# The last token block's key scans move into the last loop, with a third buffer for the second factors

## The chip, the cores and the metric

The kernel runs on one core of one Trainium2 chip. The metric is the time of one execution in device microseconds (us). The times of the kernel before are 2137.34, 2130.71 and 2142.05 us; their median is 2137.34 us.

## The reference, cut to what matters

One layer of a hybrid encoder: a mixer (HGRN2 and Hyena branches), then PEER, a retrieval among 128 x 128 single-neuron experts. The change touches PEER alone. For 512 tokens in blocks of 128:

```python
def block(xb):                                   # xb: 128 tokens x 1024
    qh = (xb @ w_q).reshape(T, 8, 2, 128)        # 8 heads, two halves each
    s = einsum('thpc,hpnc->thpn', qh, subkeys)   # 128 scores per half-head
    s1, i1 = top_k(s[:, :, 0], 16)
    s2, i2 = top_k(s[:, :, 1], 16)
    cand_s = s1[..., :, None] + s2[..., None, :] # 16 x 16 pairs
    top_s, pos = top_k(cand_s, 16)
    experts = take(i1 * 128 + i2, pos)
    g = softmax(top_s)
    u, v = u_tab[experts], v_tab[experts]        # 16,384 x 1024 tables
    act = gelu(einsum('td,thkd->thk', xb, u)) * g
    return einsum('thk,thkd->td', act, v)
```

The result is added to the residual and normed once more. All of it is float32.

## The kernel before, in words

The program is written by hand as nested generators. The order of the code sets priorities; a planner then orders each engine's queue by these priorities and by its own estimate of when operands and buffers are ready, so an instruction can be queued ahead of code that stands before it. Each queue is worked off in order. A pool's `bufs` is the number of buffers a name has; a new tile waits until the last reader of the buffer that it takes over is done. Matrices are split into a high and a low part (`split`, L83 to L86: ACT casts the high part, DVE or POOL subtracts), and each product is three products of parts (`mm3`, L89 to L97).

The four token blocks are treated in two ways. Block 0 (`GTB`) is *gathered*: for each of its 128 chosen pairs (8 heads x 16) a row of the u table per token is fetched by an indirect DMA of POOL and dotted with the token on DVE (L924), then a row of the v table is fetched and summed with its weight (L933). Blocks 1 to 3 (`DTB`) are *dense*: all 128 rows of 128 experts go through PE. A dense row's first product (`act_row`: uT row times the tokens, 24 products of 384 columns) and ACT's gelu give half of a pair `gact`; the second part (`combine`, 18 products of 512 columns) multiplies gated gacts with the v row into PSUM.

PEER runs in these stages:

- `projected` makes the normed tokens. Then `queries` (L1079) walks over 16 half-heads (head and half): it loads and splits a weight (`wlo` on DVE), projects, has PE make the scores of all four blocks, copies them by ACT into `s` (L1093), and has DVE scan each block with `top16` (L1239): the eight best, their indices, a copy without them (`rest`), the next eight, their indices, five operations per block. From half-head 8 on it takes one step after each half-head of the early selections (`chosen`, which is `select`) of the first two dense blocks.
- The gate stage finishes the dense selections and, in `gates_out`, makes for each token a 128 x 128 matrix of gates from one-hot products, which goes out to `Gd` in DRAM. A `fill` of dense first products is woven in: 2 x `KEPT` + `RING` - `LEFT` rows, 27. Of these pairs, `KEPT` are sent to DRAM (`kept`) and the others wait in the `ring`, which has `RING` / 2 + 1 buffers of one pair.
- The last loop weaves two generators: `rows` walks over the 128 dense rows and gives a weight per row, 6.0 for the first two and 2.25 for the others; `gathered` takes one step per unit of weight. `rows` does the dense first products still open (three ahead, 98 in the loop), splits v rows three ahead (`split_v`: SP loads `vraw`, ACT casts `vh`, DVE subtracts `vl`), multiplies pairs with their gates (`gated`: `gact` times `gt`, then `gh` and `gl`; a kept pair is first fetched into `gkept`) and combines. `gathered` does block 0's two selections (7 steps each, with the pool `slw2` of one buffer per name), turns the expert numbers into `gidx` (L912), and then takes one gather per step, 256 in all. In the loop POOL also does `ul`, the low part of the u rows, and all loads of `uraw`, `vraw`, `gt` and `gkept` are issued by SP, in one queue.
- The residual is added, normed and sent out.

Of the kernel before, what the change touches and what calls it, by code (L numbers as in the profile page):

```python
# [9 lines left out]
F32 = mybir.dt.float32  # L10
# [11 lines left out]
P = 128  # L22
L = 512
D = 1024
KB = D // P
TB = L // P
HEADS = 8
# [50 lines left out]
def run(gen):  # L78
    for _ in gen:
        pass  # L80


def split(nc, hi, lo, src, eng=None):  # L83

    nc.scalar.copy(hi, src)  # L85
    return (eng or nc.vector).tensor_sub(lo, src, hi).ins  # L86
# [49 lines left out]
def proj(C, src, xh, xl, eng=None):  # L136

    hi, lo = load_w(C, src, eng=eng)
    ps = C.ps_mm.tile([P, L], F32, name="ps_mm")
    mm3(C.nc, ps, [((hi[:, k], lo[:, k]), (xh[:, k], xl[:, k])) for k in range(KB)])  # L140
    return ps
# [17 lines left out]
def block_kernel(tc, a):  # L159

    nc = tc.nc
    with ExitStack() as ctx:
        const = ctx.enter_context(tc.tile_pool(name="const", bufs=1))
        ident = const.tile([P, P], F32, name="ident")
        ones = const.tile([P, P], F32, name="ones")
        nc.vector.memset(ones, 1.0)
        vec = const.tile([P, NVEC], F32, name="vec")
        nc.scalar.dma_start(vec, a["vec"])
        nc.scalar.dma_start(ident, a["ident"])
        epsc = const.tile([P, 1], F32, name="epsc")  # L170
        nc.vector.memset(epsc, EPS)
        C = Ctx()
        C.nc, C.tc, C.a, C.ident, C.ones, C.vec, C.eps = nc, tc, a, ident, ones, vec, epsc
        C.outer = ctx
        dp = ctx.enter_context(tc.tile_pool(name="dram", bufs=1, space=DRAM))
        C.Gd = dp.tile([12, P, P * 32], F32, name="Gd")
        C.hd = dp.tile([L, D], F32, name="hd")
        C.kept = dp.tile([KEPT, P, 2, ND], F32, name="kept")
        mh, ml = mixer(C)
        with ExitStack() as pctx:  # L180
            peer(C, pctx, mh, ml)
# [604 lines left out]
GTB = 0  # L786
DTB = (1, 2, 3)
ND = len(DTB) * P
T0 = DTB[0] * P
RING = 16  # L790
KEPT = 7
LEFT = 3
UB = 2
EARLY = 2
# [15 lines left out]
def peer(C, ctx, mh, ml):  # L810
    nc, tc, a = C.nc, C.tc, C.a
    cp = ctx.enter_context(tc.tile_pool(name="prc", bufs=1, side="right"))
    xh = cp.tile([P, KB, L], F32R, name="pxh")
    xl = cp.tile([P, KB, L], F32R, name="pxl")
# [3 lines left out]
    v16 = cp.tile([P, TB, 16, TOPK], F32, name="v16")  # L818
    i16 = cp.tile([P, TB, 16, TOPK], U32, name="i16")
# [10 lines left out]
    def chosen(pool, tb, part, ahead=2):  # L830
        return select(C, pool, tb, part, v16, i16, gate, eid, pio, ahead)

    projected(C, mh, ml, xh, xl, xg)
    rowctx = ExitStack()
    ring = rowctx.enter_context(tc.tile_pool(name="ring", bufs=RING // 2 + 1, side="right"))
    puctx = ExitStack()
    pu = puctx.enter_context(tc.tile_pool(name="pu", bufs=UB, side="right"))
    acts, factors, looping = {}, {}, []
    anchor = [None]
    last_gelu = [None]  # L840
# [11 lines left out]
    def act_row():  # L852

        r = order.pop(0)
        if r not in factors:
            split_u(r)
        if order:
            split_u(order[0])
        uh, ul = factors.pop(r)
        pa = C.ps_row.tile([P, 512], F32, name=C.ps_row_name)  # L860
        mm3(nc, pa[:, :ND], [((uh[:, k], ul[:, k]), (xh[:, k, T0 : T0 + ND], xl[:, k, T0 : T0 + ND])) for k in range(KB)])
        if r % 2 == 0:
            acts[r // 2] = ring.tile([P, 2, ND], F32, name="gact")
        g = acts[r // 2]
        last_gelu[0] = nc.scalar.activation(g[:, r % 2], pa[:, :ND], AF.Gelu_apprx_tanh).ins  # L865
        if r % 2 and r // 2 in kept:
            nc.scalar.dma_start(C.kept[kept.index(r // 2)], acts.pop(r // 2))

    NP = NK // 2
    kept = [p for p in range(NP) if (p + 1) * KEPT // NP > p * KEPT // NP]  # L870
    order = [r for r in range(NK) if r // 2 in kept] + [r for r in range(NK) if r // 2 not in kept]

    def act_rows():
        for _ in range(2 * KEPT + RING - LEFT):
            act_row()
            yield

    fill = act_rows()
    C.ps_row, C.ps_row_name = C.ps_mm, "ps_mm"
    queries(C, xh, xl, v16, i16, chosen, fill)  # L880
    C.wctx.close()
    C.ps_row, C.ps_row_name = ctx.enter_context(tc.tile_pool(name="ps_a", bufs=2, space=PSUM)), "ps_a"
    with tc.tile_pool(name="slw", bufs=2) as sw, tc.tile_pool(name="gb", bufs=1) as gb, \
# [10 lines left out]
    pv = rowctx.enter_context(tc.tile_pool(name="pv", bufs=2))  # L894
    swctx = ExitStack()
    sw = swctx.enter_context(tc.tile_pool(name="slw2", bufs=1))
# [4 lines left out]
    def gather(gp, tab, j):  # L901
        t = gp.tile([P, D], F32, name="grow")
        with tc.issue_after(anchor[0]):
            nc.gpsimd.indirect_dma_start(out=t, out_offset=None, in_=tab,  # L904
                                         in_offset=bass.IndirectOffsetOnAxis(ap=gidx[:, j : j + 1], axis=0))
        return t

    def gathered():

        yield from chosen(sw, GTB, 0, 1)  # L910
        yield from chosen(sw, GTB, 1, 1)
        nc.vector.tensor_copy(gidx, eid[:, GTB])  # L912
        swctx.close()
        gp = rowctx.enter_context(tc.tile_pool(name="gp", bufs=GBUFS))
        asked = chain(((a["u"], j) for j in range(P)), ((a["v"], j) for j in range(P)))
        there = [gather(gp, *q) for q in islice(asked, GAHEAD)]

        def row():
            there.extend(gather(gp, *q) for q in islice(asked, 1))
            return there.pop(0)  # L920

        for j in range(P):
            t = row()
            nc.vector.scalar_tensor_tensor(t, t, 1.0, xg, op0=ALU.mult, op1=ALU.mult, accum_out=gdot[:, j : j + 1])  # L924
            yield 1.2
        nc.scalar.activation(gw, gdot, AF.Gelu_apprx_tanh)
        nc.vector.tensor_mul(gw, gw, gate[:, GTB])
        for j in range(P):
            t = row()
            if j == 0:  # L930
                nc.vector.tensor_scalar(gacc, t, gw[:, 0:1], None, op0=ALU.mult)
            else:
                nc.vector.scalar_tensor_tensor(gacc, t, gw[:, j : j + 1], gacc, op0=ALU.mult, op1=ALU.add)  # L933
            yield 1.2
# [1 line left out]
    prep = {}  # L936

    def split_v(r):
        raw = pv.tile([P, D], F32, name="vraw")
        nc.sync.dma_start(raw, a["v"][r * P : r * P + P])  # L940
        vh = pv.tile([P, D], F32R, name="vh", bufs=AHEAD + 1)
        vl = pv.tile([P, D], F32R, name="vl", bufs=AHEAD + 1)
        split(nc, vh, vl, raw)
        prep[r] = vh, vl
# [69 lines left out]

    looping.append(True)
    weave(rows(), gathered(), 1.0)


# [57 lines left out]
    C.woctx.close()  # L1076


def queries(C, xh, xl, v16, i16, chosen, fill):  # L1079

    nc, tc, a = C.nc, C.tc, C.a
    with tc.tile_pool(name="slc", bufs=1) as cp, tc.tile_pool(name="slw0", bufs=2) as w2, tc.tile_pool(name="slw1", bufs=2) as sw:
        sk = cp.tile([P, 16, P], F32, name="sk")
        nc.scalar.dma_start(sk, a["skT"])

        def scores(hp, ps):
            qT = w2.tile([P, L], F32, name="qT")
            nc.scalar.copy(qT, ps)
            pt = C.ps_x.tile([P, 512], F32, name="ps_x")
            for tb in range(TB):  # L1090
                nc.tensor.matmul(pt[:, tb * P : tb * P + P], qT[:, tb * P : tb * P + P], sk[:, hp], start=True, stop=True)
            s = w2.tile([P, TB, P], F32, name="s")
            nc.scalar.copy(s, pt.rearrange("p (t n) -> p t n", t=TB))  # L1093
            for tb in DTB + (GTB,):
                top16(C, w2, v16[:, tb, hp], i16[:, tb, hp], s[:, tb])

        early = chain(*(chosen(sw, tb, 0) for tb in DTB[:EARLY]))
        for hp in range(16):
            scores(hp, C.first[hp] if hp < 2 else proj(C, a["w_q"][hp], xh, xl))
            if hp > 7:  # L1100
                run(islice(early, STEPS))
        run(early)
        for _ in range(2):
            next(fill)
# [134 lines left out]
def top16(C, pool, val, idx, src):  # L1239

    nc = C.nc
    rest = pool.tile(list(src.shape), F32, name="rest", tag=f"rest{src.shape[-1]}")
    nc.vector.max(val[:, 0:8], src)
    nc.vector.max_index(idx[:, 0:8], val[:, 0:8], src)
    nc.vector.match_replace(rest, val[:, 0:8], src, NEG)
    nc.vector.max(val[:, 8:16], rest)
    nc.vector.max_index(idx[:, 8:16], val[:, 8:16], rest)
# [111 lines left out]
```

## Time and profile before

| what | value |
|---|---|
| median of three runs | 2137.34 us (2130.71 to 2142.05) |
| the profiled execution | 2140.67 us, span 2138.9 us |
| PE busy | 2061.9 us, 96% |
| DVE busy | 1697.0 us, 79% |
| ACT busy | 962.4 us, 45% |
| POOL busy | 617.1 us, 29% |
| HBM traffic over the span | 189 GB/s |

Busy time is the share of the span in which an engine works on something; matmuls overlap in the records, so a busy PE need not be a PE at its peak. Where an engine was idle, the profile names what ended the wait. SPq is SP's queue of DMA issues. A name such as `vl` stands for all buffers of that name.

### The profile page before, as it was taken

How to read it: one execution, taken by the hardware profiler on the slowest of the kernel's cores; microseconds unless marked ns; L12 is line 12 of the kernel's file. 1: busy time of each engine (PE TensorE's matmuls, PEld its weight loads, DVE VectorE, ACT ScalarE, POOL GpSimd, SP SyncE). 2: the span in 40 equal slices, each digit the busy share in tenths (PEclk: the TensorE clock that was granted, in tenths of full speed). 3: DMA queues.
4: the chain of work that ended last, by engine and by line, in shares of the span. 5: the costliest groups of instructions: out<-in, count | busy, mean ns of one | idle time of the engine just before them, and what ended most of it. 6: DMA issues, size and time to landing. Idle time of an engine off the chain costs nothing.

```text
span 2138.9 us, 29773 instructions
## 1 busy us (share of the span) xinstructions
PE 2061.9 (96%) x11109; PEld 1819.3 (85%) x11109; DVE 1697.0 (79%) x3073; ACT 962.4 (45%) x1382; POOL 617.1 (29%) x361
## 2 busy tenths in 40 slices
PE   7999999999999999989989999999999999999998
PEld 6888888888888898778889888899888888899987
DVE  6788765999997648999999787787777668778765
ACT  5555435666565623337776332332332323332333
POOL 0000000000000000000001566777776666677640
PEclk9999999999999999989999999999999999999999
DMA  6212222221222434124547988888898888889964
GB/s 194 82 50 65 70 69 100 62 70 60 70 63 75 137 130 139 50 72 173 202 161 245 312 287 299 309 325 309 285 324 281 301 303 313 306 292 333 316 217 158
DMA packets 153661, 406.89 MB, mean 190 GB/s; under 512 B 12425, under 2 KB 65419, under 8 KB 151852
## 3 DMA queue, kind: packets, MB, share of 16 engines
q1 hardware_dynamic: 109884, 255.59, 35.5%
q0 software_dynamic: 36864, 134.23, 17.2%
q10 hardware_dynamic: 6768, 15.17, 2.0%
q8 instruction: 87, 1.43, 0.3%
q14 instruction: 58, 0.48, 0.1%
HBM read 372.83 MB, written 32.11 MB: 189 GB/s over the span
## 4 chain that ended last, share of the span: by engine, by line
PE 56%; DVE 20%; DMA 9%; issue 7%; ACT 4%; POOL 3%; DVEq 0%; ACTq 0%; POOLq 0%; SPq 0%
PE ps_mm L97 7%; PE ps_mm L95 7%; PE ps_mm L94 7%; PE acc L973 5%; PE acc L974 4%; PE acc L972 4%; PE ps_a L94 4%; PE ps_a L97 4%; PE ps_a L95 4%; DMA grow<-in_u,gidx 3%; DMA vraw<-in_v 3%; DMA grow<-in_v,gidx 2%; PE ps_g L1228 2%; POOL grow L904 2%; PE ps_x L718 2%
## 5 line engine op out<-in xcount | busy, mean ns | idle before, releaser
L86 POOL TENSOR_TENSOR ul<-uraw,uh 128x1024 fp32r<-128x1024 f32 x100 | 257.6, 2576 | 634.2 <-DMA uraw<-in_uT 396.4
L85 ACT CAST vh<-vraw 128x1024 fp32r<-128x1024 f32 x128 | 134.7, 1053 | 597.5 <-DMA vraw<-in_v 525.0
L94 PE MATMUL ps_a<-pxh,uh 128*128 128x384 f32 x1008 | 343.9, 341 | 23.6 <-ACT gact L865 23.4
L95 PE MATMUL ps_a<-pxl,uh 128*128 128x384 f32 x1008 | 342.3, 340 | 0.0
L973 PE MATMUL acc<-vl,gh 128*128 128x512 f32 x768 | 300.7, 392 | 0.4 <-DVE vl L86 0.4
L974 PE MATMUL acc<-vh,gl 128*128 128x512 f32 x768 | 300.8, 392 | 0.0
L972 PE MATMUL acc<-vh,gh 128*128 128x512 f32 x768 | 298.8, 389 | 0.0
L933 DVE SCALAR_TENSOR_TENSOR xg<-grow,gw,xg 128x1024 f32<-128x1024 f32 x127 | 194.9, 1534 | 88.6 <-DMA grow<-in_v,gidx 87.5
L94 PE MATMUL ps_mm<-xh,whi 128*128 128x512 f32 (+1 forms) x656 | 259.4, 397 | 1.6 <-ACT xh L195 1.3
L924 DVE SCALAR_TENSOR_TENSOR grow<-grow,xg 128x1024 f32<-128x1024 f32 x128 | 189.4, 1497 | 88.5 <-DMA grow<-in_u,gidx 88.5
L95 PE MATMUL ps_mm<-xl,whi 128*128 128x512 f32 (+1 forms) x656 | 255.2, 390 | 0.3 <-DVE xl L196 0.3
L94 PEld LDWEIGHTS ps_a<-pxh,uh 128*128 128x128 f32 x1008 | 191.1, 190 | 34.1 <-ACT gact L865 30.8
L826 POOL IOTA iota<- 128x512 bf16 x1 | 1.2, 1237 | 756.5 <-DVE gt L281 756.5
L97 PE MATMUL ps_a<-pxh,ul 128*128 128x384 f32 x1008 | 200.9, 340 | 10.7 <-DVE ul L86 10.3
L86 DVE TENSOR_TENSOR vl<-vraw,vh 128x1024 fp32r<-128x1024 f32 x128 | 188.9, 1477 | 18.9 <-ACT vh L85 18.8
L904 POOL DMA_INDIRECT grow<-in_u,gidx x128 | 185.8, 1451 | 45.3 <-issue 22.4
L95 PEld LDWEIGHTS ps_a<-pxl,uh 128*128 128x128 f32 x1008 | 191.1, 190 | 3.2
L97 PEld LDWEIGHTS ps_a<-pxh,ul 128*128 128x128 f32 x1008 | 177.7, 190 | 12.9 <-DVE ul L86 12.3
L904 POOL DMA_INDIRECT grow<-in_v,gidx x128 | 172.3, 1346 | 34.8 <-issue 18.6
L85 ACT CAST whi<-wraw 128x1024 fp32r<-128x1024 f32 x112 | 117.3, 1050 | 133.1 <-PE ps_mm L95 122.6
L974 PEld LDWEIGHTS acc<-vh,gl 128*128 128x128 f32 x768 | 144.1, 188 | 30.2
L973 PEld LDWEIGHTS acc<-vl,gh 128*128 128x128 f32 x768 | 144.1, 188 | 28.9 <-DVE vl L86 0.8
(413 smaller groups left out, 4150.3 us busy)
## 6 DMA issues: line engine op xcount, KB each, us to landing
uraw<-in_uT SPq DMA_DIRECT2D x128, 512.0 KB, 6.9
vraw<-in_v SPq DMA_DIRECT2D x128, 512.0 KB, 5.5
wraw<-in_w_in SPq DMA_DIRECT2D x80, 512.0 KB, 3.6
Gd<-Gs SPq DMA_DIRECT2D x12, 2048.0 KB, 7.3
gt<-Gd SPq DMA_DIRECT2D x32, 768.0 KB, 9.4
wraw<-in_w_q SPq DMA_DIRECT2D x16, 512.0 KB, 4.3
wraw<-in_w_b SPq DMA_DIRECT2D x8, 512.0 KB, 3.6
wraw<-in_w_a SPq DMA_DIRECT2D x8, 512.0 KB, 4.3
```

Of the source, the lines that this page charges most:

```text
L85: nc.scalar.copy(hi, src)
L86: return (eng or nc.vector).tensor_sub(lo, src, hi).ins
L94: nc.tensor.matmul(out, ah, bh, start=(i == 0), stop=False)
L95: nc.tensor.matmul(out, *((al, bh) if late else (ah, bl)), start=False, stop=False)
L97: nc.tensor.matmul(out, *((ah, bl) if late else (al, bh)), start=False, stop=(stop and i == n - 1))
L718: nc.tensor.matmul(pl[:, cs], KM[:, 0, cs], KM[:, 1, cs], start=True, stop=True)
L904: nc.gpsimd.indirect_dma_start(out=t, out_offset=None, in_=tab, in_offset=bass.IndirectOffsetOnAxis(ap=gidx[:, j : j + 1], axis=0))
L924: nc.vector.scalar_tensor_tensor(t, t, 1.0, xg, op0=ALU.mult, op1=ALU.mult, accum_out=gdot[:, j : j + 1])
L933: nc.vector.scalar_tensor_tensor(gacc, t, gw[:, j : j + 1], gacc, op0=ALU.mult, op1=ALU.add)
L972: nc.tensor.matmul(acc[k][:, c], gh[:, ts_], vh[:, ds_], start=(r == 0), stop=False)
L973: nc.tensor.matmul(acc[k][:, c], gh[:, ts_], vl[:, ds_], start=False, stop=False)
L974: nc.tensor.matmul(acc[k][:, c], gl[:, ts_], vh[:, ds_], start=False, stop=(r == NK - 1))
```

## The change

The scores of block 0 are no longer scanned in `queries`. ACT copies them into a tile `s0` that holds all 16 half-heads (8 KB per partition, from the start of the queries to the end of block 0's selections), and `s` holds the three dense blocks alone. `gathered` begins with the scans: eight half-heads, two per step, then the selection of the first four heads, then the same again. A weight that a generator yields counts only in the generator that leads the weave, so the 3.2 stands for one step. `vraw` gets three buffers where it had two. `RING` goes from 16 to 14 and `KEPT` from 7 to 8.

```diff
-RING = 16
-KEPT = 7
+RING = 14
+KEPT = 8
...
+    sgctx = ExitStack()
     pu = puctx.enter_context(tc.tile_pool(name="pu", bufs=UB, side="right"))
+    s0 = sgctx.enter_context(tc.tile_pool(name="sg", bufs=1, side="right")).tile([P, 16, P], F32, name="s0")
...
-    queries(C, xh, xl, v16, i16, chosen, fill)
+    queries(C, xh, xl, v16, i16, s0, chosen, fill)
...
     def gathered():
 
-        yield from chosen(sw, GTB, 0, 1)
-        yield from chosen(sw, GTB, 1, 1)
+        for part in range(2):
+            for hp in range(part * HEADS, part * HEADS + HEADS):
+                top16(C, sw, v16[:, GTB, hp], i16[:, GTB, hp], s0[:, hp])
+                if hp % 2:
+                    yield 3.2
+            yield from chosen(sw, GTB, part, 1)
+        sgctx.close()
...
     def split_v(r):
-        raw = pv.tile([P, D], F32, name="vraw")
+        raw = pv.tile([P, D], F32, name="vraw", bufs=3)
...
-            s = w2.tile([P, TB, P], F32, name="s")
-            nc.scalar.copy(s, pt.rearrange("p (t n) -> p t n", t=TB))
-            for tb in DTB + (GTB,):
-                top16(C, w2, v16[:, tb, hp], i16[:, tb, hp], s[:, tb])
+            pt = pt.rearrange("p (t n) -> p t n", t=TB)
+            s = w2.tile([P, len(DTB), P], F32, name="s")
+            nc.scalar.copy(s, pt[:, DTB[0] : DTB[-1] + 1])
+            nc.scalar.copy(s0[:, hp], pt[:, GTB])
+            for k, tb in enumerate(DTB):
+                top16(C, w2, v16[:, tb, hp], i16[:, tb, hp], s[:, k])
```

## Rows read from the trace of the kernel before

**Rows 1.** The page: busy time, share of the span and instructions of each engine

```profile
PE 2061.9 (96%) x11109; PEld 1819.3 (85%) x11109; DVE 1697.0 (79%) x3073; ACT 962.4 (45%) x1382; POOL 617.1 (29%) x361
```

**Rows 2.** Windows: length, busy us (count) of PE, PEld, DVE, ACT, POOL; clock, DMA share, GB/s

```profile
820.00:865.40 45.40, 45.40 (x227) 37.57 (x226) 45.09 (x260) 15.76 (x22) 0.00 (x0) 1.00 0.35 105
865.40:1143.40 278.00, 251.89 (x1602) 231.05 (x1601) 275.21 (x918) 173.46 (x285) 0.00 (x0) 0.97 0.39 143
...
1205.00:1215.00 10.00, 10.00 (x50) 8.87 (x50) 7.25 (x9) 2.50 (x4) 8.24 (x7) 1.00 1.03 404
1206.00:2076.00 870.00, 853.23 (x4234) 765.24 (x4232) 655.78 (x606) 279.51 (x351) 586.30 (x345) 1.00 0.86 304
```

**Rows 3.** Waits of PE, 865.4 to 1143.4: total us, times, longest us

```profile
PE ps_a L97 <- DVE ul L86: 10.3, 4, 7.9
```

**Rows 4.** Timeline of DVE in the queries: start us, length us, instruction

```profile
854.02 1.21 DVE L86 TENSOR_TENSOR wlo<-wraw,whi 128x1024 fp32r<-128x1024 f32 x1
...
860.09 1.21 DVE L86 TENSOR_TENSOR wlo<-wraw,whi 128x1024 fp32r<-128x1024 f32 x1
...
865.43 0.21 DVE L1134 CAST i16f<-i 128x128 f32<-128x128 uint32 x1
```

**Rows 5.** Timeline of ACT in the queries; in brackets the idle time before, and its end

```profile
854.07 0.59 ACT L1093 COPY s<-ps_x 128x512 f32<-128x512 f32 x1 [1.29 <-PE ps_x L1091]
...
860.54 0.59 ACT L1093 COPY s<-ps_x 128x512 f32<-128x512 f32 x1 [1.29 <-PE ps_x L1091]
```

**Rows 6.** Waits of PE for gact, from 1165 us on, and from 1200 us on

```profile
PE ps_a L94 <- ACT gact L865: 21.5, 14, 3.9
...
PE ps_a L94 <- ACT gact L865: 17.6, 13, 2.4
```

**Rows 7.** Timelines of DVE and PE at the entry of the last loop

```profile
1143.40 0.23 DVE L1134 CAST i16f<-i 128x128 f32<-128x128 uint32 x1 [0.69 <-PE ps_g L1228]
...
1169.40 0.49 PE L94 MATMUL ps_a<-pxh,uh 128*128 128x384 f32 x1 [3.90 <-ACT gact L865]
...
1199.14 0.22 DVE L912 CAST gidx<-eid 128x128 int32<-128x128 f32 x1
```

**Rows 8.** Waits of ACT, 1165 us to the end: the longest sum

```profile
ACT vh L85 <- DMA vraw<-in_v: 525.0, 96, 16.7
```

**Rows 9.** Waits of SP's queue, 1165 to 2100 us: the longest sum

```profile
SPq L940 <- DVE vl L86: 661.0, 119, 13.9
```

**Rows 10.** Timelines of ACT, POOL, PE and DVE around one stall of the last loop

```profile
1233.77 1.05 ACT L85 CAST vh<-vraw 128x1024 fp32r<-128x1024 f32 x1 [3.84 <-DMA vraw<-in_v]
...
1235.84 2.93 POOL L86 TENSOR_TENSOR ul<-uraw,uh 128x1024 fp32r<-128x1024 f32 x1 [1.95 <-ACT uh L85]
...
1236.21 0.44 PE L94 MATMUL ps_a<-pxh,uh 128*128 128x384 f32 x1 [2.05 <-ACT gact L865]
...
1236.45 3.40 DVE L86 TENSOR_TENSOR vl<-vraw,vh 128x1024 fp32r<-128x1024 f32 x1
```

**Rows 11.** DVE by shape, whole span: out<-in xcount | busy us, mean ns | idle before

```profile
L1247 DVE FIND_INDEX8 i<-v,rest 128x8 uint32<-128x128 f32 x64 | 18.5, 289 | 0.0
...
L1246 DVE MAX8 ctop<-rest 128x8 f32<-128x50 f32 x32 | 6.5, 202 | 0.1
```

**Rows 12.** DVE by line, last loop alone (1175 to 2093 us)

```profile
L86 DVE TENSOR_TENSOR vl<-vraw,vh 128x1024 fp32r<-128x1024 f32 x120 | 177.2, 1478 | 12.3 <-ACT vh L85 12.2
L959 DVE TENSOR_TENSOR gact<-gact,gt 128x768 f32<-128x768 f32 x55 | 67.3, 1225 | 10.3 <-DMA gt<-Gd 10.1
L86 DVE TENSOR_TENSOR gl<-gact,gh 128x768 fp32r<-128x768 f32 x55 | 65.5, 1190 | 0.0
...
L1246 DVE MAX8 ctop<-rest 128x8 f32<-128x50 f32 x4 | 0.8, 203 | 0.0
```

**Rows 13.** Timeline of DVE at the end: last gathered rows, first sums of PE's results

```profile
2073.04 2.60 DVE L933 SCALAR_TENSOR_TENSOR xg<-grow,gw,xg 128x1024 f32<-128x1024 f32 x2
...
2123.10 1.29 DVE L1028 TENSOR_TENSOR ht<-ht,acc 128x512 f32<-128x512 f32 x2 [5.85 <-PE acc L974]
```

More of the change, by code (lines that the diff above doesn't have):

```diff
@@ L1076, in projected, with queries @@
     C.woctx.close()
-def queries(C, xh, xl, v16, i16, chosen, fill):
+def queries(C, xh, xl, v16, i16, s0, chosen, fill):
     nc, tc, a = C.nc, C.tc, C.a
```

## The prediction

> **What bounds the kernel now.** I went from the page's share of each engine to windows cut at the stage borders, then to the waits of PE, of ACT and of SP's queue, and last to the timeline at the borders. On the page the reader is to see PE busy 2061.9 of the span's 2138.9 us [rows 1]: what can be won is PE's idle time, 77 us, and only where it lies. Two places of it are touched here.
>
> The first is the stretch from 865.4 to 1143.4 us, where pairs are selected and the dense blocks' gates are written out. DVE is busy 275.21 of 278.00 us there and PE 251.89 [rows 2], so DVE sets the end and PE has 26.1 us of idle; its longest sum of waits is for DVE's ul, 10.3 us in 4 [rows 3]. From 820 to 865.4 both look full [rows 2], but the timeline separates them: DVE takes 6.07 us from one half-head's wlo to the next (854.02 to 860.09) [rows 4], while ACT copies scores, as PE delivers them, 6.47 us apart (854.07 to 860.54) [rows 5]. The wlo gains on the copy from 0.05 to 0.45 us ahead, so in the first eight of 16 half-heads PE is the slower one. At 865.43 the first early selection begins on DVE [rows 4], and from there DVE has more to do than PE.
>
> The second is the last loop. From 1206 to 2076 us PE is busy 853.23 of 870.00 us at a granted clock of 1.00, DVE 655.78 us (75%), and the DMA engines 0.86 at 304 GB/s [rows 2]. PE is the bound, and its waits are nearly all of one sort, for gact, ACT's gelu: 21.5 us in 14 from 1165 on, of which 17.6 in 13 lie after 1200, none over 2.4 us [rows 6]; the other one, 3.90 us, is the entry [rows 7]. ACT is not loaded: it sat 525.0 us before vh until vraw landed [rows 8], with the gelu behind vh in its queue. SP, which issues vraw, sat 661.0 us in 119 waits for DVE's vl, the last reader of a vraw buffer [rows 9]. One case: ACT gets vraw at 1233.77 after 3.84 us, casts, runs the gelu, and PE goes on at 1236.21 after 2.05 us idle [rows 10].
>
> **The change part by part.** The sum is made against the profiled execution, 2140.67 us (span 2138.9 and 1.8 around it). It lies 3.3 us above the median of 2137.34, inside the spread of the three runs (2130.71 to 2142.05).
>
> *The gathered block's 16 scans leave the query stage.* Of a half-head's 6.07 us on DVE, wlo is 1.21 [rows 4]; four scans of five operations share the other 4.86, 1.215 us each. (By its duration one operation takes up to 0.289 us [rows 11] and a scan 1.45; successive ones overlap, so starts are the better measure.) Sixteen are 19.4 us. In the first eight half-heads PE sets the pace and nothing gets shorter. In the other eight DVE is behind without a break, and all that follows up to 1143.4 us moves ahead by 8 x 1.215 = 9.7 us. Bounds: 19.4 us, if DVE was the bound from the start; nothing, if the planner puts these scans, ready long before, back among the gate work. I take 9.7, because DVE is full there and PE has 26.1 us of idle to give. What is late next in that stretch is still DVE.
>
> *ACT copies scores in two pieces.* Sixteen copies of 128 x 128 are added, and a row of 128 x 512 took 0.59 us [rows 5], so under 9 us; the other piece gets shorter. ACT is busy 15.76 of 45.40 us in that stage [rows 2] and idle 1.29 us before each copy until PE is done [rows 5], which hides it: zero. If that cover goes, at most 0.59 us per half-head.
>
> *The scans come back at the entry of the last loop.* Before, DVE spends 55.8 us between the end of the gates (1143.40) and gidx (1199.14) [rows 7], on two selections and the first rows' factors. In code order the eight added yields move the first gather from row 2.9 of the loop to row 6.4: the first two rows take 6 steps each, every further row 2.25, and there are 22 steps ahead of the gathers where there were 14. A row's own work on DVE is 2.7 us: one vl of 1.48 and half of a pair's gact product and gl, 1.2 [rows 12]. So DVE reaches gidx 55.8 + 19.4 + 3.5 x 2.7 = 85 us after the gates. PE makes 4234 products in 870 us [rows 2], 0.2055 us each; a row with its dense partner has 24 + 18 of them, 8.6 us. It came to the loop 26 us after the gates (1169.40) [rows 7], so it is at row 6.4 after 26 + 55 = 81 us. DVE comes 4 us late, against factors that are split three rows (26 us) ahead. Before, by the same count, it was 5 us late (55.8 against 26 + 25), and PE did not wait there beyond the 3.90 us. Bounds: nothing, to 23 us (16 scans of 1.45 us, end to end, as their single rest buffer may force, on PE's path). I take 2, near the row of before.
>
> *The later gathers.* The last sum of a gathered row ended at 2075.6, and the last additions waited for PE until 2123.1 [rows 13]. 3.5 rows of 8.6 us later is 2106 on the old axis, 17 us short of PE's end: zero. If that cover went, each us beyond would count.
>
> *A third buffer for vraw.* A load can be issued a row sooner, 7.7 us on the mean (98 dense rows over 120 steps make 37.6 products a step). No stall in the loop is over 2.4 us, so where DMA has room each is covered; where the engines are full (1.03 at 404 GB/s from 1205 to 1215) [rows 2], a load issued earlier only queues earlier. Bounds: nothing to 17.6 us. I take two thirds, 12 us, because the mean share is 0.86, nearer to full than to free, yet the wait for vl stands in 119 of 128 loads.
>
> *Ring shorter by a pair, an eighth kept pair.* The fill stays at 27 dense rows (2 x 8 + 14 - 3), the entry does 3 and the loop 98, as before; counted through the code, a ring buffer is still used again no sooner than three rows after its release. One more pair of 384 KB goes out and comes back, 1.3 us of DMA each way at 304 GB/s, hidden. On SP's queue one more gkept, with its one buffer, may hold a vraw behind it, by no more than the longest wait there, 13.9 us [rows 9], against the row (7.7 us) now in hand: zero, up to 6 us if it meets a late one.
>
> Sum: 2140.67 - 9.7 - 12 + 2 = 2121; less the 3.3 us by which this execution lay above the median, 2117.7. I say 2118.
>
> **Two rules of the skill.** In the loop, DVE operations on two SBUF operands stretch beside POOL: vl took 3.40 us at 1236.45, while POOL's ul ran from 1235.84 for 2.93 us [rows 10]; its mean is 1478 ns there [rows 12]. The scans of one operand do not: 203 ns in the loop [rows 12], 202 over all [rows 11]. The Trainium skill says so in SBUF — State Buffer, § Who interferes with whom: a DVE instruction with two SBUF inputs and a GpSimd instruction that reads SBUF shut each other out, one with a single input is untouched. By it the moved scans cost the same 19.4 us in the loop; held up like vl they would cost 24. The page DMA: Bandwidth & Descriptors of the Trainium skill, § Where 436 GB/s comes from, speaks against the buffer: HBM gives a core about 358 GB/s, and 304 is 85% of that. The 404 GB/s of the row above stands over its figure, so the trace gives the loop more room than the page does.
>
> **The rivals.**
> A. *The buffer is hidden by DMA.* vraw is late because the DMA engines are full, and the stalls stay. For it: the share of 0.86, and 96 times that ACT waited for vraw [rows 8]. Against it: SP issues vraw only after vl in 119 cases [rows 9]. Time: 2137.3 - 9.7 + 2 = 2129.6.
> B. *The scans move and free nothing.* The planner's new order holds PE as long as before up to 1143. Against it: DVE is full there [rows 2]. Buffer alone: 2137.3 - 12 + 2 = 2127.3.
> C. *Both come in full.* 2137.3 - 9.7 - 17.6 = 2110; with some of the first eight half-heads' scans counted, 2104.
> D. *Slower: the entry of the loop starves.* The scans stand on DVE ahead of the first gact products, gl and vl; ACT's gh and the gelu behind it wait, and PE with them, as in the 3.90 us at 1169.40 [rows 7]. Price: 23 us on the path, less 9.7, with the buffer's gain used up by the transfers that bunch up behind it: 2137.3 + 13 = 2150. It decides once DVE is more than 26 us late at row 6.4, 22 more than I count. For it: the wait at the entry is there already. Against it: with 5 us of delay PE lost nothing more.
>
> **How the numbers follow.** Forecast (2112 to 2125) 0.42, C 0.14, A 0.18, B 0.14, D 0.12. A measurement can tell about 0.5%, 10.7 us, from no change, so faster means below 2126.6: the forecast, C and a third of A and B, which lie within 3 us of that line, 0.66. Within: the rest of A and B and a little of D, 0.24. Slower: 0.10. The range leaves out some of C and most of D: 2106 to 2139.
>
> **What would show it.** Right: DVE's end of the gates (1143.4) comes about 10 us sooner; SP's 661 us for vl shrink by hundreds, and PE's 17.6 us for gact fall to about 6; gidx comes some 30 us later after the loop's start than now, with no gap of PE over 4 us before the first gather. Wrong: the gates end where they did (first step); the waits for gact stay, with DMA at 0.86 or more (buffer); PE waits for vl, gh or gact around the new scans (entry); or the last gathered row is summed after PE's last product.

## The result, and the profile after

The changed kernel takes 2113.90 us (median of 5 runs, 2113.02 to 2115.41), a ratio of 0.9895 to the kernel before (95% interval 0.9871 to 0.9918). The forecast was 2118 us, in 2106 to 2139. Run once more with the later experiments it gave 2113.16 us, 0.9886 (0.9865 to 0.9906). The profiled executions stand 26.8 us apart (spans 2138.9 and 2112.1).

All comparisons of traces below use three borders: the first score product of the queries, the gates' end (DVE's last product `own` begins), and PE's last product. They lie at 818.8, 1140.9 and 2130.8 us before, at 818.4, 1131.9 and 2104.2 us after. So the stages in front became 8.6 us shorter (322.1 to 313.5), the rest 17.6 us (989.9 to 972.3). Line numbers after are 2 to 10 higher than before (L972 to L974 are now L979 to L981).

Windows of the kernel after (columns as in [rows 2]): the queries, the gate stage, the whole rest, the entry of the loop, and its two halves:

```profile
818.40:915.40 97.00, 93.88 (x469) 77.68 (x468) 91.44 (x515) 31.64 (x60) 0.00 (x0) 0.99 0.21 66
915.40:1131.90 216.50, 201.15 (x1351) 191.49 (x1351) 214.94 (x572) 154.70 (x258) 0.00 (x0) 0.96 0.48 176
1131.90:2104.20 972.30, 965.37 (x4801) 869.68 (x4800) 801.21 (x892) 350.54 (x428) 636.80 (x356) 0.99 0.84 297
1158.00:1168.00 10.00, 7.67 (x26) 6.68 (x27) 10.00 (x12) 7.31 (x9) 4.64 (x2) 0.66 0.50 163
1221.10:1631.00 409.90, 407.23 (x2023) 366.67 (x2023) 332.63 (x365) 143.82 (x170) 317.09 (x174) 1.00 0.90 321
1631.00:2061.60 430.60, 430.60 (x2152) 388.67 (x2152) 359.48 (x245) 152.86 (x180) 294.10 (x174) 1.00 0.87 309
```

The same window of the rest in the kernel before:

```profile
1140.90:2130.80 989.90, 967.89 (x4803) 868.49 (x4802) 749.28 (x802) 333.04 (x428) 615.63 (x356) 1.00 0.83 292
```

Length less busy time is PE's idle time: 22.0 us before, 6.9 after. In the loop's second half PE has no gap left. The waits of PE in that stretch after, where [rows 6] had 14 for gact:

```profile
PE acc L979 <- ACT vh L85: 2.6, 1, 2.6
PE ps_a L97 <- POOL ul L86: 2.2, 1, 2.2
PE acc L980 <- DVE vl L86: 2.1, 2, 1.6
```

ACT now waits for PE, and little for vraw [rows 8]; SP waits for vl about as long as ever [rows 9] (667.4 us before in the same stretch). ACT's waits, then SP's:

```profile
ACT vh L85 <- PE acc L981: 179.7, 54, 3.6
...
ACT vh L85 <- DMA vraw<-in_v: 70.7, 13, 10.9
```

```profile
SPq L947 <- DVE vl L86: 651.4, 121, 12.2
```

DVE's scan operations on `s` and `s0` (one name in the trace) from the first score product to the gates' end. The three dense blocks have 48 of each kind, so block 0 still has 14 first maxima and 12 index searches here; of its 80 operations 54 left the stage:

```profile
L1254 DVE FIND_INDEX8 i<-v,s 128x8 uint32<-128x128 f32 x60 | 17.2, 288 | 0.0
L1253 DVE MAX8 v<-s 128x8 f32<-128x128 f32 x62 | 16.1, 283 | 5.4 <-ACT s L1102 5.4
L1255 DVE MATCH_REPLACE8 rest<-v,s 128x128 f32<-128x128 f32 x48 | 13.4, 279 | 0.0
```

### The profile page after: what moved, and what is told of

Its sections match the earlier page's. It is cut to its first block, busy times and chain, and to the rows that moved or that the text cites. A ratio compares the mean times of both kernels' runs of the same rounds, so it can differ in the third digit from the quotient of the medians.

```text
span 2112.1 us, 29790 instructions
## 1 busy us (share of the span) xinstructions
PE 2058.7 (97%) x11109; PEld 1822.7 (86%) x11109; DVE 1736.1 (82%) x3073; ACT 978.6 (46%) x1396; POOL 638.2 (30%) x361
## 3 DMA queue, kind: packets, MB, share of 16 engines
q0 software_dynamic: 36864, 134.23, 17.6%
## 5 line engine op out<-in xcount | busy, mean ns | idle before, releaser
L86 POOL TENSOR_TENSOR ul<-uraw,uh 128x1024 fp32r<-128x1024 f32 x100 | 265.3, 2654 | 589.7 <-DMA uraw<-in_uT 387.6
L979 PE MATMUL acc<-vh,gh 128*128 128x512 f32 x768 | 299.7, 390 | 2.6 <-ACT vh L85 2.6
L981 PE MATMUL acc<-vh,gl 128*128 128x512 f32 x768 | 301.5, 393 | 0.0
L940 DVE SCALAR_TENSOR_TENSOR xg<-grow,gw,xg 128x1024 f32<-128x1024 f32 x127 | 208.6, 1643 | 63.1 <-DMA grow<-in_v,gidx 62.0
L931 DVE SCALAR_TENSOR_TENSOR grow<-grow,xg 128x1024 f32<-128x1024 f32 x128 | 195.9, 1541 | 73.6 <-DMA grow<-in_u,gidx 73.3
L906 POOL DMA_INDIRECT grow<-in_u,gidx x128 | 201.0, 1570 | 41.4 <-issue 19.4
L85 ACT CAST uh<-uraw 128x1024 fp32r<-128x1024 f32 x128 | 134.7, 1053 | 143.5 <-PE ps_a L95 76.5
```

The costliest lines, as they stand in the source:

```text
L979: nc.tensor.matmul(acc[k][:, c], gh[:, ts_], vh[:, ds_], start=(r == 0), stop=False)
L981: nc.tensor.matmul(acc[k][:, c], gl[:, ts_], vh[:, ds_], start=False, stop=(r == NK - 1))
```

## The experiments

Each kernel is compared with runs of the kernel before on its own chip. The 12 runs were made on more than one chip, where the kernel before had medians of 2135.5 to 2140.9 us, so ratios are what compares across groups.

**The parts one by one.** *Buffer*: the kernel before with the third buffer and the new ring, no scan moved.

```diff
-RING = 16
-KEPT = 7
+RING = 14
+KEPT = 8
...
-        raw = pv.tile([P, D], F32, name="vraw")
+        raw = pv.tile([P, D], F32, name="vraw", bufs=3)
```

> The third vraw buffer with RING 14 and KEPT 8, the scans left in the query stage. Theory (two separate gains that add: the scans shorten the stage that DVE bounds, the buffer takes the loop's stalls): 2122 us (2118 to 2127), ratio about 0.993; the gates end as before, within 2 us of 1141; ACT's wait for vraw falls from 525 us to under 120, PE's wait for gact in the loop from 17.6 to under 4 us. Rival (the loop got free because the gathers come later and in less crowded transfers, not because of the buffer): within 4 us of before, ACT's wait for vraw over 400 us.

2117.49 us, 0.9896 (0.9868 to 0.9925): more than I expected. The rest takes 966.5 us, 23.4 less than before:

```profile
1141.30:2107.80 966.50, 962.62 (x4805) 868.67 (x4803) 780.37 (x802) 351.76 (x428) 640.06 (x356) 1.00 0.84 299
```

Idle fell from 22.0 to 3.9 us (18.1), and the same products took 5.3 us less busy time. DMA moves 299 GB/s where it moved 292, and a vraw lands no sooner after its issue (median 6.2 us; 5.5 before), but ACT's wait for vraw is 53.6 us where it was 525.0: the engines had room for the earlier loads.

*Ring*: the ring alone (the two constants above).

> RING 14 and KEPT 8 alone. Theory: no change, 2137 us within 4, gact waits in the loop still 12 to 20 us. Rival (the new ring makes the planner lay the loop out in another way, and that is part of the gain): 5 us or more faster, with gact waits under 10 us.

2145.03 us, 1.0026 (1.0000 to 1.0052), at the edge of what I allowed. The new ring brings nothing by itself and may cost some 5 us beside two buffers. The ring of 16 with three buffers was not run, so the new ring's price there stays open.

*Scans*: the changed kernel with two vraw buffers.

> The changed kernel with vraw back at two buffers (scans moved, RING 14, KEPT 8). Theory: 2128 us (2124 to 2132), ratio about 0.996; the gates end 9 us sooner than before, PE's waits for gact in the loop stay at 12 to 20 us and ACT's for vraw over 400 us. Rival (the relief of DVE is the whole gain): 2114 us, like the changed kernel. Rival (the scans at the entry cost as much as they free): 2137 us.

2151.22 us, 1.0063 (1.0040 to 1.0086): a miss, and on the other side of the kernel before. *Scans16* puts the old ring back as well, so that only the scans are moved (against the changed kernel):

```diff
-RING = 14
-KEPT = 8
+RING = 16
+KEPT = 7
...
-        raw = pv.tile([P, D], F32, name="vraw", bufs=3)
+        raw = pv.tile([P, D], F32, name="vraw")
```

> The scans moved alone, with two vraw buffers and the ring of 16 with 7 kept pairs as in the kernel before. Theory one, the entry is what the moved scans cost and the old ring takes the rest of the loss away: 8.6 us gained at the gates, about 6 given back at the entry, 2135 to 2139. Theory two, late vraw loads and the scans meet at the entry whatever the ring, as in the scans kernel (6 us above the kernel before with the short ring, 2 with that ring's 4 taken off): 2142 to 2148.

2146.75 us, 1.0043 (1.0023 to 1.0062): theory two. The scans alone make the kernel slower, though its gates end 9.3 us sooner after the first score product (312.8). The rest, and PE's waits in it:

```profile
1130.50:2138.90 1008.40, 977.39 (x4801) 875.15 (x4800) 775.31 (x892) 333.72 (x428) 621.24 (x356) 0.98 0.81 286
```

```profile
PE ps_a L94 <- ACT gact L867: 18.8, 12, 3.7
PE acc L980 <- DVE vl L86: 7.2, 3, 5.6
```

It is 18.5 us longer than before, half by idle time (31.0 against 22.0) and half by longer busy time (977.4 against 967.9), at a granted clock of 0.98. With three buffers the same move costs the rest 5.8 us (972.3 against 966.5).

*Half*: the changed kernel, with block 0's first eight scans left in the queries.

```diff
-            for hp in range(part * HEADS, part * HEADS + HEADS):
+            for hp in range(HEADS, 2 * HEADS) if part else ():
...
+            if hp < HEADS:
+                top16(C, w2, v16[:, GTB, hp], i16[:, GTB, hp], s0[:, hp])
```

> The changed kernel, but the gathered block's first eight half-heads are scanned in the query stage again; only the other eight move. Theory (PE sets the pace in the first eight, so moving these gains nothing): 2114 us within 3, the gates end within 1.5 us of the changed kernel's, gidx some 10 us sooner. Rival (DVE was the bound from the start): half of the stage's gain is lost, the gates end 4 to 5 us later, 2118 to 2119 us.

2111.91 us, 0.9870 (0.9842 to 0.9899). The gates end 313.9 us after the first score product against 313.5: the first eight scans had gained nothing there.

**Is vraw late because DMA is full?** *Novgather*: the kernel before, with 127 of the 128 gathers of v rows left out; the sums take one row again and again.

```diff
-        asked = chain(((a["u"], j) for j in range(P)), ((a["v"], j) for j in range(P)))
+        asked = chain(((a["u"], j) for j in range(P)), ((a["v"], j) for j in range(1)))
...
-            t = row()
+            if j == 0:
+                t = row()
```

> The kernel before, without 127 of the 128 gathered rows of v: the sums use one row over and over, so only DMA load is taken from the loop's second half, about 0.5 MB every 8.6 us falls to half. Theory one (prediction's rival A: vraw is late because the DMA engines are full): ACT's waits for vraw in the second half fall by more than half, and PE's gact stalls after the last u row is gathered (1650 us) vanish. Theory two (the load is issued too late, for SP waits for vl): ACT still waits for vraw about as often, shorter by under a third, and some stalls after 1650 us stay.

One run: 2179.66 us, which neither theory had. The sums, no longer paced by gathers, fill DVE until 1907.5 us. That stretch here, and in the kernel before:

```profile
1640.40:1907.50 267.10, 236.34 (x1113) 205.99 (x1111) 264.18 (x183) 71.42 (x90) 67.53 (x24) 0.96 0.40 127
```

```profile
1640.40:1907.50 267.10, 261.83 (x1304) 235.10 (x1303) 201.41 (x145) 88.16 (x111) 177.62 (x106) 1.00 0.86 306
```

ACT's waits for vraw from 1640 to 1907 us here, and in the kernel before:

```profile
ACT vh L85 <- DMA vraw<-in_v: 153.2, 23, 10.0
```

```profile
ACT vh L85 <- DMA vraw<-in_v: 149.8, 25, 14.0
```

With DMA at 0.40 instead of 0.86, ACT waits for vraw as long. That alone doesn't clear DMA, for the edit also filled DVE (264.18 of 267.10 us), whose vl a load's issue waits for. But once the sums are done, DVE is over half free while DMA has a share of 0.48, and ACT's waits for vraw (here from 1907 to 2130 us) nearly vanish:

```profile
1907.50:2169.80 262.30, 258.77 (x1260) 231.14 (x1260) 112.49 (x87) 95.44 (x123) 58.94 (x24) 0.99 0.48 149
```

```profile
ACT vh L85 <- DMA vraw<-in_v: 11.2, 2, 8.8
```

Within this run the wait goes with DVE and not with DMA's share, as it should if a load is late because it is issued late, behind vl. That the DMA engines had room at 0.86 is shown by buffer, not by this run.

**Where the ring costs.** *Kept2*: the ring kernel with a second buffer for gkept.

```diff
-            g = pv.tile([P, 2, ND], F32, name="gkept", bufs=1)
+            g = pv.tile([P, 2, ND], F32, name="gkept", bufs=2)
```

> As the ring kernel (two vraw buffers, no scan moved, ring of 14 with 8 kept pairs), with a second buffer for gkept. Theory one, the 4 us that the ring kernel lay above the kernel before come from gkept's single buffer, which holds vraw loads behind it on SP's queue: SP's waits for DVE's gl ahead of gkept (36.4 us in 7 there) fall to under 5, and the time goes back to 2138, within 3. Theory two, they come from the ring itself or from chance: the waits fall, and the time stays at 2143, within 3.

2150.06 us, 1.0053 (1.0025 to 1.0081). SP's waits for gl didn't fall (33.6 us in 6; 36.4 in 7 in the ring kernel), so the edit did not take away what it was to test, and why the ring costs beside two buffers stays open.

**What the entry costs.** *Again*: the changed kernel, for comparison.

> The changed kernel once more, beside the others of this group. Both theories: 2114 us, within 3. It is here so that the next kernels are compared with it on one chip.

2113.16 us. *Halflate*: the half kernel with six empty steps before the gathered work.

```diff
     def gathered():
+        for _ in range(6):
+            yield
```

> As the half kernel (eight of the gathered block's scans stay in the queries, eight move), but the gathered work takes its first step in the loop six steps later. Theory one, the price at the entry is DVE's work standing ahead of the first gact product: the first product of the loop comes 6 us sooner after the gates than in the half kernel (38.5 us there), and the time falls to 2107, within 3. Theory two, the planner sets DVE's order whatever the code order of these steps, so the first product moves by under 2 us: 2112, within 3. A loss over 4 us would say that the gathered rows, some 20 us later, then reach the end of the loop.

2112.13 us, 0.9881 (0.9859 to 0.9903). The first product of the loop comes 37.6 us after the gates (38.5 in half), and PE waits 7.0 us for gact (6.9): theory two. The planner left DVE's work ahead of that product where it was; gidx came 77.0 us after the gates' end, only 4.8 later than in half.

*Behind*: the changed kernel, with the moved scans bound behind the first row's vl.

```diff
-                top16(C, sw, v16[:, GTB, hp], i16[:, GTB, hp], s0[:, hp])
+                with tc.issue_after(first[0]): top16(C, sw, v16[:, GTB, hp], i16[:, GTB, hp], s0[:, hp])
...
-    prep = {}
+    prep, first = {}, []
...
-        split(nc, vh, vl, raw)
+        first.append(split(nc, vh, vl, raw))
```

> The changed kernel, with the 16 moved scans held behind the first row's vl of the last loop, so that none of their operations runs in the query or gate stage and none ahead of the loop's first gact product, gl and vl. Theory one, the changed kernel loses 7 us at the loop's entry because DVE's scans stand ahead of the first factors, and left a third of the scans' operations in the earlier stages: gates end another 3 to 6 us sooner, PE waits under 4 us in all at the entry, gidx comes some 20 us later, nothing is lost at the end: 2104, within 4. Theory two, DVE is simply full at the entry and its work has to be done somewhere: the waits come back a few rows later for vl, gl or the exponentials in ACT's queue, as long as before: 2113, within 3.

2114.50 us, 0.9887 (0.9860 to 0.9913): no faster. From the gates' end at 1131.4 to 1234.8 us PE is never idle, so the order of DVE's queue was the price of the first rows. But gidx comes at 1234.8 us, and POOL's queue has gathers ahead of a ul. PE's only wait in the rest, and POOL's timeline at that place (start, length, instruction):

```profile
PE ps_a L97 <- POOL ul L86: 10.2, 1, 10.2
```

```profile
1235.27 1.09 POOL L906 DMA_INDIRECT grow<-in_u,gidx  x1 [7.61 <-DVE gidx L919]
...
1249.78 2.35 POOL L86 TENSOR_TENSOR ul<-uraw,uh 128x1024 fp32r<-128x1024 f32 x1
```

Nine gathers stand between the two. All 80 scan operations left the earlier stages here, and these took 313.4 us, as in the changed kernel (313.5): the last 26 gained nothing.

*Halfheld*: the half kernel, with scans and selections bound behind the first vl (the scans and `first` as in behind).

```diff
+    def held(gen):
+        for go in iter(int, 1):
+            with tc.issue_after(first[0]): c = next(gen, None)
+            if c is None: return
+            yield c
...
-            yield from chosen(sw, GTB, part, 1)
+            yield from held(chosen(sw, GTB, part, 1))
```

> As the half kernel, but the eight moved scans and both selections of the gathered block are held behind the first row's vl of the last loop. Theory one (the order of DVE's queue is the price): gates end as in the half kernel, the 6.9 us that PE waited for gact at the entry there shrink to under 2, 2105, within 3. Theory two (DVE is full whatever the order): 2112, within 3, with PE waiting for vl or gl after the first rows.

2124.92 us, 0.9942 (0.9919 to 0.9965). The wait for gact went (0.4 us), but gidx came 92.1 us after the gates' end (72.2 in half), and PE waits 20.5 us for a ul: neither theory. *Behind6*: the behind kernel with the first gathers six steps later.

```diff
         nc.vector.tensor_copy(gidx, eid[:, GTB])
+        for _ in range(6): yield 1.2
```

> As the behind kernel, with the first gathers six steps (some 23 us) later in code order, so that one more ul, the twelfth of the loop, stands ahead of them on POOL's queue. Theory one, in the behind kernel the time won at the loop's entry was lost again because POOL's first gather waits for gidx with the next ul behind it, and PE behind that for 10.2 us: that wait falls under 2 us, and the time is 2103, within 3. Theory two, the late selection is paid for in any case: another wait (for ul again, for vl, or the last gathered rows at the end) takes its place, 2110 or more.

2111.96 us, 0.9877 (0.9855 to 0.9898). One more ul runs ahead of the gathers, and PE still waits 7.2 us, for the one after it: theory two. Behind6, half, halflate and the changed kernel (0.9870 to 0.9895) can't be told apart.

## Why the prediction was right, step by step

**The scans leave the queries: 9.7 forecast, 8.6 measured**, with DVE still full in the gate stage (214.94 of 216.50 us) and no gain from the first eight, as half shows. What I had listed only as a bound happened in part: the planner put 26 of the 80 operations back among earlier work, those that need no `rest` buffer. It cost nothing, as behind shows. Of the 26, 14 lie before 864 us, where PE sets the pace. The other 12 lie where I took DVE for the bound; in behind, without them, DVE is idle for 10.8 us of the stages in front instead of 7.1, and nothing is gained. So DVE is no longer the only bound there, though I had said that it stays what is late next.

**ACT's copies: zero, as forecast.** They take 0.48 and 0.27 us by the trace, where one took 0.59 [rows 5].

**The entry of the loop: 2 forecast, 5.8 measured**, within the bounds. The trace of after shows two places. The first is the first row: ACT's exponentials of the new selection stand in its queue ahead of gh and vh (start, length, instruction, idle before it):

```profile
1156.00 0.26 ACT L1169 ACTIVATE ex<-ex 128x64 f32<-128x64 f32 x1 [6.43 <-DVE ex L1168]
1156.87 0.83 ACT L85 CAST gh<-gact 128x768 fp32r<-128x768 f32 x1 [0.61 <-DVE gact L966]
1157.61 1.99 ACT L85 CAST vh<-vraw 128x1024 fp32r<-128x1024 f32 x2
```

DVE, with scans and selection first, lets ACT wait 6.43 us; PE waits 2.6 us for vh and 1.6 for vl, and from 1158 to 1168 us has a clock of 0.66. But these 4.2 us take the place of the 3.9 us that PE waits for gact in the buffer kernel, as before [rows 7]. The second place is the first gather (POOL's timeline, then PE's):

```profile
1221.59 1.54 POOL L906 DMA_INDIRECT grow<-in_u,gidx  x1 [9.68 <-PE ps_a L97]
...
1228.12 2.35 POOL L86 TENSOR_TENSOR ul<-uraw,uh 128x1024 fp32r<-128x1024 f32 x1
```

```profile
1230.53 2.53 PE L97 MATMUL ps_a<-pxh,ul 128*128 128x384 f32 x8 [2.18 <-POOL ul L86]
```

This ul had its uh from ACT at 1213.0 us, but five gathers stand ahead of it, and the first of them waits for gidx. (The profile names a product of PE; gidx was done at 1221.30, 0.29 us before the gather, as it was 0.28 us before it in the kernel before.) Idle time in the rest is 3.0 us more than in the buffer kernel: 2.2 for this ul, 0.5 for a later vl, and only 0.3 at the first row. Busy time is 2.8 us more, and the clock covers it: busy time times the missing clock, summed over windows of 5 us, is 4.1 us in after and 1.5 in buffer, and some 1.5 us of the 4.1 follow this wait. So my count of rows looked near the right place, the first gather, but asked only whether DVE's factors are late there; late was POOL's ul, behind the gathers, a path that is in neither my sum nor a rival. Rival D named the wait of the first row, which hardly grew. The scan operations themselves didn't stretch, as forecast: three that run beside a ul of POOL, from 1143.75 us on, take 0.28 to 0.29 us.

**The later gathers: zero, as forecast.** gidx came 89.2 us after the gates' end, 31.0 more than before (29 forecast), and the last sum ended 42.6 us ahead of PE's last product (I had said 17).

**The third buffer: 12 forecast, 23 measured, past my bound of 17.6.** This is the term that was mis-sized, and the others hid it. All of the loop's stalls for gact behind the entry went, not two thirds: I cut them because I took 0.86 of DMA for nearly full, and buffer shows that it had room. The rule of the Trainium skill that spoke against the buffer (DMA: Bandwidth & Descriptors, § Where 436 GB/s comes from: some 358 GB/s from HBM for a core) did not come to bear: the changed loop's first half moves 321 GB/s at a share of 0.90, and PE has 2.7 us of idle there. The 5.3 us of busy time beyond the stalls I did not count at all. Part of it is the clock. Two stalls of before, and the windows around them:

```profile
1624.05 0.69 PE L94 MATMUL ps_a<-pxh,uh 128*128 128x384 f32 x1 [2.41 <-ACT gact L865]
...
1737.92 0.39 PE L973 MATMUL acc<-vl,gh 128*128 128x512 f32 x1
1738.14 0.39 PE L974 MATMUL acc<-vh,gl 128*128 128x512 f32 x1
1740.73 0.45 PE L94 MATMUL ps_a<-pxh,uh 128*128 128x384 f32 x1 [2.19 <-ACT gact L865]
1741.01 0.34 PE L95 MATMUL ps_a<-pxl,uh 128*128 128x384 f32 x1
1741.19 0.35 PE L94 MATMUL ps_a<-pxh,uh 128*128 128x384 f32 x1
```

```profile
1621.00:1626.00 5.00, 2.59 (x9) 2.14 (x8) 3.31 (x2) 4.38 (x6) 2.31 (x1) 0.76 1.04 331
1738.00:1743.00 5.00, 2.81 (x16) 2.38 (x15) 2.02 (x2) 4.71 (x6) 2.49 (x1) 1.00 0.64 213
```

After the first gap PE runs on for a while at the lower of its two clock levels, 1.2 instead of 2.4 GHz (a product of 384 columns every 0.32 us instead of 0.18), after the second it doesn't. The missing clock, summed as above, is 2.4 us before, 1.5 in buffer and 11.2 in scans16. So the clock explains about 1 us of buffer's 5.3 and most of the 9.5 by which scans16 is busier than before. Most of the other 4 us lies at the edges of the gaps, as the second one shows: the last product before it runs its 0.39 us alone, where the next one otherwise starts 0.22 us after it, and the first one behind it is followed after 0.28 us instead of 0.18. By these rows a gap adds some 0.27 us of busy time, an estimate of 3.5 us for the 13 that went; what remains, under 1 us, stays open.

**Ring and kept pair: zero forecast**, up to 6; 1.0026 measured beside two buffers (4.1 us by the medians), not measured beside three.

**One sign that I named was wrong.** SP's 661 us for vl were to shrink by hundreds, and they are 651.4. SP issues in order and ahead of time: with another buffer it runs one row further and then waits as long. The sign was in ACT's wait for vraw, 525.0 to 70.7 us.

In the profiles the terms are 8.6 less in front, 23.4 less by the buffer and 5.8 more by the scans, 26.2 of the 26.8 us (forecast 19.7). They add up because the buffer kernel is taken as the step between. That the time came within about 4 us of 2118 is in part luck: the buffer was worth 11 us more than I said, the gates and the entry together 5 us less, and 2113.90 is as near to rival C's 2110. By ratio the scans bring nothing that can be told beside the buffer (0.9895 and 0.9886 against 0.9896); without it they cost 0.4%. So the two parts are not separate gains: with the new ring the buffer takes the ratio from 1.0026 to 0.9896 where the scans stay, and from 1.0063 to 0.9895 where they move. That the scans win at the gates what they lose in the loop I had only as rival D, in which the buffer's gain went too.

## What to carry to other kernels

When a prefetch buffer is added, read its worth from the consumer's wait for the data and from the gaps of the engine that sets the pace, not from the issuing queue's wait, which only moves ahead. A mean DMA share says little on whether an earlier load helps; ask what the issue waits for. Work moved to an engine with idle time is paid at the place where its queue is full, and through every queue that holds an instruction waiting for it: here ACT's exponential, then POOL's gather.

## What was not expected of the hardware

A late gather at the head of POOL's queue cost PE more than late factors: halfheld's 20.5 us without products, with 22.1 us of POOL waiting for gidx. Times scatter with the number of buffers: 22 runs of the kernel before beside buffer's lie between 2131.2 and 2150.2 us, buffer's 6 between 2116.3 and 2119.1; 12 of scans16 between 2138.7 and 2155.6, 6 of the changed kernel between 2109.9 and 2115.3. Whether the many stalls of 1 to 4 us make the scatter was not tested.
